# Routing queries without the last norm factor, relu ahead of the split, and lower routing rates

## The chip, the core and the metric

The kernel runs on one core of a Trainium2 chip. The metric is the device time of one execution in microseconds (us). Before the change the median of three runs is 1587.6 us (1587.5 to 1587.79). The engines are TensorE (PE; PEld is its weight load), VectorE (DVE), ScalarE (ACT), GpSimd (POOL), and SyncE (SP), whose queue issues most of the loads.

## What is computed

256 tokens of width 1024 pass three layers. Cut to what matters here:

```python
# layers 0 and 1: attention, layer norm, then
h = layer_norm(ALPHA * h + jnp.square(jax.nn.relu(h @ w_up)) @ w_down)   # width 4096
# layer 0's attention ends with a norm over each head of 128
o = o * lax.rsqrt(jnp.mean(o * o, axis=-1, keepdims=True) + LN_EPS)
# hybrid layer
mixed = concat([rmsnorm(o_a, out_gain_a), rmsnorm(o_b, out_gain_b)]) @ w_out
h = x + mixed
xt = rmsnorm(h, norm2_gain)
# peer: 8 heads, each key 2 x 128 wide, 16384 experts
q = _rms((xt @ w_q).reshape(T, 8, 256))
s1, s2 = q[..., :128] . sub_keys[:, 0], q[..., 128:] . sub_keys[:, 1]
v1, i1 = top_k(s1, 16); v2, i2 = top_k(s2, 16)
vals, ci = top_k(v1[:, None] + v2[None, :], 16)         # 16 experts per head
g = softmax(vals)
y = sum over chosen experts e: g_e * gelu(xt . u_e) * v_e
out = h + y
```

The routing norm divides each query head by its own root mean square, and `rmsnorm(h)` is a factor per token times `h` times a gain per column.

## The kernel before

**Products and blocks.** Every float32 product is made of three matmuls on a high and a low half of each operand (hi*hi, hi*lo, lo*hi). A weight block of 128 x 1024 is loaded by SP's queue into `raw` (four buffers). ACT casts the high half `whi` (L415), and DVE subtracts to get the low half `wlo` (L417); both go to a pool of split blocks, `w` (three buffers) and for the layers up to the hybrid one `wx` (three more). `pump` does that split as soon as a split buffer is free, so the cast of a block waits for the matmuls of an earlier block.

**A projection by features** (`proj_F`, L479) takes eight such blocks, one per 128 columns of the input, and for each issues 24 matmuls of 256 columns: eight hi*hi (L490), then pairs of lo*hi and hi*lo (L494, L495). After each block it calls a hook, pumps, and lets one step of the background list `bg` (`tick`) be issued. Its result fills four PSUM banks of 512 columns. The last block of a group is issued by pairs of outputs, so that the banks end one after another.

**Order.** Each engine takes its instructions in program order. Where the code is plain, that is the order in which the Python lines run. In the hybrid layer `Flow` sets it: many small generators, each added with a rank (`f.add(step, rank)`), say what engine they want next, for how long, and which events they wait for; a list scheduler picks among those that are ready by time and rank, and issues dummy matmuls on PE (L1292, `fill`) where its own estimate finds PE idle.

**Up projection** (`mlp`, L809). Four groups of `proj_F`; at each group's end four banks are relued (ACT, L830), squared (DVE, L831), cast to the high half (ACT, L554) and subtracted (DVE, L555), then `pump` splits the next blocks.

**Sub-norm** (`sub_norm`, L914). Layer 0's attention squares eight pieces of 128 columns on ACT with an accumulator (L920), then takes the root.

**End of the hybrid layer.** `out_dense` (L2030) multiplies the two mixers' outputs with `w_out`: part "b" first, part "a" last, sixteen steps of three matmuls, over four PSUM banks (two token halves th, two column halves i). `last_rms` (L2070) makes the factor `ra` of the first mixer's norm. Then `H.rms` adds the four banks to h (DVE, L2143), squares h on ACT (L2145), makes the root (L382 and what follows it on DVE), scales (`xn`, L2154), transposes on PE (L561, two times eight), and splits the transposed columns into the halves of x by pairs of ACT (L584) and DVE (L585). h is stored to `hscr`.

**Peer** (L2163). Two groups of `proj_F` make the routing queries (P.q). `score_steps`, run from `bg`, scores them against the sub keys and collects the sums of squares `ssq`. Then sixteen groups of `proj_F` (P.U) make xt . u for all experts. In its hooks `routing()` (L2257) issues top-k work on DVE: each step yields a cost, and each hook issues steps until the sum of costs reaches the sum of the rates so far (L2379). In routing stage 0 the low half of the weights is made by POOL (`self.lo_eng = nc.gpsimd`), and by DVE from the end of that stage on. Stage changes hold an exp (L2293) with two table loads on ACT; at each group's end ACT evacuates four banks with Gelu (L2403).

## Time and profile before

| | us |
|---|---|
| median of three runs | 1587.6 |
| profiled execution | 1586.47 |
| its span | 1584.7 |
| PE busy | 1551.7 |
| DVE busy | 1127.3 |
| ACT busy | 823.5 |
| POOL busy | 147.7 |

Busy time is counted from the first to the last moment of an instruction, matmuls that run at half clock included. A row of the list in order of time gives the start, the busy time, the engine, the line, the operation, output and inputs, and a count where equal rows are merged; in brackets stands the idle time before it and what ended that. Stages in us from the start of the span: the sub-norms around 100, the group ends of layer 0's up projection 160 to 230 and of layer 1's up to 542, the hybrid layer 612 to 755, `H.rms` to 766, P.q to about 815, P.U to 1234, and P.V behind it.

### The profile page before, as it was taken

To read this page: it belongs to the slowest core of one execution; us is meant where nothing else is said; L and a number is where in the kernel's file an instruction comes from. 1 tells how busy PE (TensorE), PEld (TensorE's weight loads), DVE (VectorE), ACT (ScalarE), POOL (GpSimd) and SP (SyncE) were. 2 spreads that over 40 slices of the span, in tenths; PEclk is the share of its full clock that TensorE was granted. 3 is DMA by queue.
4 is the path that set the end of the run, shared out by engine and by line. 5 is a ranking of instruction groups with operands and counts; after the bars stand their busy time and mean duration, and the time that the engine had idled before them with its cause. 6 is when DMAs were issued, how large, how long until landed. Compare 5 with 4: busy or idle time off the path is not lost.

```text
span 1584.7 us, 26875 instructions
## 1 busy us (share of the span) xinstructions
PE 1551.7 (98%) x10433; PEld 1393.8 (88%) x10433; DVE 1127.3 (71%) x2172; ACT 823.5 (52%) x1304; POOL 147.7 (9%) x114
## 2 busy tenths in 40 slices
PE   8989999999999999999999998999999999999999
PEld 8879998897799887787999998999999888888887
DVE  5668666586686757777536998778887666666666
ACT  5564555356465654557455444555555544544443
POOL 2000000000200003000027880000000000000000
PEclk9999999999999999999999999999999999999999
DMA  8535768663578695961455775766665777777774
GB/s 295 206 107 173 258 245 286 228 209 124 134 237 292 213 330 205 322 219 49 160 151 184 240 226 190 237 191 209 175 198 176 257 246 246 232 250 237 241 246 153
DMA packets 100306, 339.85 MB, mean 214 GB/s; under 512 B 11121, under 2 KB 16577, under 8 KB 100177
## 3 DMA queue, kind: packets, MB, share of 16 engines
q1 hardware_dynamic: 91216, 310.09, 59.6%
q10 hardware_dynamic: 5760, 18.58, 3.0%
q0 software_dynamic: 3200, 9.45, 2.1%
q8 instruction: 82, 1.34, 0.3%
q14 instruction: 48, 0.39, 0.1%
HBM read 303.74 MB, written 34.34 MB: 213 GB/s over the span
## 4 chain that ended last, share of the span: by engine, by line
PE 71%; DVE 15%; DMA 5%; ACT 5%; issue 2%; SPq 0%; ACTq 0%; DVEq 0%
PE ps L475 13%; PE ps L477 13%; PE ps L476 13%; PE ps L490 9%; PE ps L494 9%; PE ps L495 9%; DVE wlo L417 2%; PE ps L2344 2%; ACT whi L415 2%; DMA ahead<-w_in 1%; DVE t L2253 1%; DMA pre<-ahead 1%; DVE t L2248 1%; DVE t L2251 1%; DVE t L2250 1%
## 5 line engine op out<-in xcount | busy, mean ns | idle before, releaser
L415 ACT CAST whi<-raw 128x1024 fp32r<-128x1024 f32 (+1 forms) x454 | 473.2, 1050 | 498.9 <-PE ps L477 205.2
L417 DVE TENSOR_TENSOR wlo<-raw,whi 128x1024 fp32r<-128x1024 f32 x410 | 498.3, 1223 | 289.4 <-ACT whi L415 288.7
L494 PE MATMUL ps<-x,wlo 128*128 128x256 f32 x1920 | 476.8, 284 | 4.7 <-DVE wlo L417 4.5
L495 PE MATMUL ps<-x,whi 128*128 128x256 f32 x1920 | 476.1, 284 | 0.0
L494 PEld LDWEIGHTS ps<-x,wlo 128*128 128x128 f32 x1920 | 369.2, 192 | 5.7 <-DVE wlo L417 5.7
L495 PEld LDWEIGHTS ps<-x,whi 128*128 128x128 f32 x1920 | 369.4, 192 | 0.0
L490 PE MATMUL ps<-x,whi 128*128 128x256 f32 x1920 | 290.9, 287 | 10.1 <-ACT whi L753 5.9
L475 PE MATMUL ps<-whi,x 128*128 128x512 f32 (+1 forms) x738 | 290.1, 393 | 0.8 <-ACT x L554 0.5
L477 PE MATMUL ps<-whi,x 128*128 128x512 f32 (+1 forms) x738 | 286.2, 388 | 1.5 <-DVE x L1376 1.4
L476 PE MATMUL ps<-wlo,x 128*128 128x512 f32 (+1 forms) x738 | 285.6, 387 | 0.3 <-DVE wlo L420 0.3
L490 PEld LDWEIGHTS ps<-x,whi 128*128 128x128 f32 x1920 | 254.0, 192 | 11.8 <-ACT whi L753 5.9
L475 PEld LDWEIGHTS ps<-whi,x 128*128 128x128 f32 x738 | 138.6, 188 | 34.1 <-issue 5.3
L477 PEld LDWEIGHTS ps<-whi,x 128*128 128x128 f32 x738 | 138.6, 188 | 32.3 <-DVE x L1376 2.6
L476 PEld LDWEIGHTS ps<-wlo,x 128*128 128x128 f32 x738 | 138.7, 188 | 27.7 <-DVE wlo L420 0.6
L417 POOL TENSOR_TENSOR wlo<-raw,whi 128x1024 fp32r<-128x1024 f32 x44 | 106.6, 2422 | 71.2 <-ACT whi L415 71.1
L476 PE MATMUL ps<-wlo,hid 128*128 128x512 f32 x256 | 100.8, 394 | 0.2 <-DVE wlo L417 0.2
L477 PE MATMUL ps<-whi,hid 128*128 128x512 f32 x256 | 100.6, 393 | 0.0
L475 PE MATMUL ps<-whi,hid 128*128 128x512 f32 x256 | 100.6, 393 | 0.0
L476 PEld LDWEIGHTS ps<-wlo,hid 128*128 128x128 f32 x256 | 48.1, 188 | 11.6 <-DVE wlo L417 0.7
L475 PEld LDWEIGHTS ps<-whi,hid 128*128 128x128 f32 x256 | 48.1, 188 | 10.9
L477 PEld LDWEIGHTS ps<-whi,hid 128*128 128x128 f32 x256 | 48.1, 188 | 10.8
L2358 DVE TENSOR_TENSOR oh<-iota,rt 128x1024 f16<-128x1024 f16 x64 | 44.1, 690 | 16.5 <-PE ps L2344 16.3
(397 smaller groups left out, 1462.3 us busy)
## 6 DMA issues: line engine op xcount, KB each, us to landing
raw<-peer_uT SPq DMA_DIRECT2D x128, 512.0 KB, 3.7
raw<-peer_v SPq DMA_DIRECT2D x128, 512.0 KB, 4.3
raw<-w_up SPq DMA_DIRECT2D x64, 512.0 KB, 5.1
raw<-w_down SPq DMA_DIRECT2D x64, 512.0 KB, 5.0
spill<-ga SPq DMA_DIRECT2D x30, 512.0 KB, 6.1
ga<-spill SPq DMA_DIRECT2D x30, 512.0 KB, 5.4
raw<-w_in_a SPq DMA_DIRECT2D x23, 512.0 KB, 5.7
raw<-w_kv SPq DMA_DIRECT2D x16, 512.0 KB, 5.2
```

Of the source, the lines that this page charges most:

```text
L415: (self.hi_eng or nc.scalar.copy)(out=hi[:, :n], in_=raw[:, :n])
L417: eng.tensor_tensor(out=lo[:, :n], in0=raw[:, :n], in1=hi[:, :n], op=ALU.subtract)
L475: mm(out=out, lhsT=lh, rhs=rh, start=start, stop=False, skip_group_check=skip)
L476: mm(out=out, lhsT=lh, rhs=rl, start=False, stop=False, skip_group_check=skip)
L477: mm(out=out, lhsT=ll, rhs=rh, start=False, stop=stop, skip_group_check=skip)
L490: mm(out=outs[o], lhsT=hi[:, sl], rhs=xs.hi(k), start=k == 0 and o % 2 == 0, stop=False, skip_group_check=True)
L494: mm(out=outs[o], lhsT=lo[:, sl], rhs=xs.hi(k), start=False, stop=False, skip_group_check=True)
L495: mm(out=outs[o], lhsT=hi[:, sl], rhs=xs.lo(k), start=False, stop=k == K - 1, skip_group_check=True)
L2248: nc.vector.max_index(out=idx[:, 0:8], in_max=vals[:, 0:8], in_values=src)
L2250: nc.vector.match_replace(out=wk, in_to_replace=vals[:, 0:8], in_values=src, imm_value=-HUGE)
L2344: nc.tensor.matmul(out=o, lhsT=oh[:, t // 2, 0, :, t % 2], rhs=b[:, t // 2, i, :, t % 2], start=i == 0, stop=i == 1)
L2358: nc.vector.tensor_tensor(out=oh.rearrange("p q i n t -> p (q i) n t"), in0=iota.unsqueeze(1).to_broadcast([P, 4, P, 2]), in1=rt[:, 0, pr] ...
```

## The change

1. `mlp`: relu and square of bank j are issued before the split of bank j-1, in both layers.
2. `sub_norm`: two squares of 512 columns on ACT and two reductions on DVE in place of eight squares with an accumulator.
3. `Flow`: ranks change; the last two steps of each bank of part "a" are issued bank by bank (`skew`); the four last updates of h are a generator of the flow (`last_update`).
4. `H.rms`: the 26 dummy matmuls of `fill(8.0)` go; the transposes take h without the factor; squares and root come after the split of x, and give `r2`.
5. Peer: queries and sums of squares are made from x without the factor. `ssq` is multiplied by `r2` twice and `rq` once. `row_of_factors`, the first step in `bg`, turns `r2` into a row of factors `rr` (two DVE scalings `rb`, two matmuls, an ACT copy), and in the second query group each pair of x's chunks is joined, multiplied by `rr` and split again in place (`renorm`).
6. `rates` go from (2.6, 1.0, 1.6) to (2.45, 1.0, 1.65).

```diff
@@ -825,11 +825,15 @@
             for g in range(4):
                 self.ahead_on = True
                 acc = self.proj_F(self.xs, hook=pause if g == 3 else None)
-                for j in range(4):
-                    y = mp.tile([P, 512], F32, tag="relu", name="relu", bufs=3)
-                    nc.scalar.activation(out=y, in_=acc[j], func=AF.Relu)
-                    nc.vector.tensor_tensor(out=y, in0=y, in1=y, op=ALU.mult)
-                    self.split_x(hid, g * 8 + 2 * j, 2, y.rearrange("p (c t) -> p c t", t=S))
+                ys = []
+                for j in range(5):
+                    if j < 4:
+                        y = mp.tile([P, 512], F32, tag="relu", name="relu", bufs=3)
+                        nc.scalar.activation(out=y, in_=acc[j], func=AF.Relu)
+                        nc.vector.tensor_tensor(out=y, in0=y, in1=y, op=ALU.mult)
+                        ys.append(y)
+                    if j:
+                        self.split_x(hid, g * 8 + 2 * (j - 1), 2, ys[j - 1].rearrange("p (c t) -> p c t", t=S))
...
@@ -913,20 +917,17 @@
 
             def sub_norm(hg):
                 ss = self.st.tile([P, 2, 4], F32, tag="ss", name="ss", bufs=2)
+                ns = [ap.tile([P, 512], F32, tag="on", name="on", bufs=4) for _ in range(2)]
                 for th in (1, 0):
-                    for h in range(4):
-                        junk = ap.tile([P, P], F32, tag="junk", name="junk", bufs=2)
-                        ol = o[hg][th][:, h * P:(h + 1) * P]
-                        nc.scalar.activation(out=junk, in_=ol, func=AF.Square, accum_out=ss[:, th, h:h + 1])
+                    nc.scalar.activation(out=ns[th], in_=o[hg][th], func=AF.Square)
+                    nc.vector.tensor_reduce(out=ss[:, th], in_=ns[th].rearrange("p (h d) -> p h d", d=P), axis=AX.X, op=ALU.add)
                 r = self.st.tile([P, 2, 4], F32, tag="sr", name="sr", bufs=2)
                 self.rsqrt_act(r.rearrange("p a b -> p (a b)"), ss.rearrange("p a b -> p (a b)"), LN_EPS, 1.0 / P)
-                ns = []
                 for th in range(2):
-                    n = ap.tile([P, 512], F32, tag="on", name="on", bufs=4)
+                    n = ns[th]
                     nc.vector.tensor_tensor(
                         out=n.rearrange("p (h d) -> p h d", d=P), in0=o[hg][th].rearrange("p (h d) -> p h d", d=P),
                         in1=r[:, th].unsqueeze(2).to_broadcast([P, 4, P]), op=ALU.mult)
-                    ns.append(n)
...
-            f.add(out_dense("a", range(4), end - 4, a_last), 5)
-            f.add(mla_update(), 7.5)
-            f.add(last_rms(), 8)
+            f.add(out_dense("a", range(4), end - 4, a_last), 4.5)
+            f.add(mla_update(), 6.5)
+            f.add(last_rms(), 3.5)
+            f.add(last_update(), 4.5)
...
             def out_dense(which, ks, b, last):
-                for n, k in enumerate(ks):
-                    for th in range(2):
-                        for i in range(2):
-                            ev = yield on_pe(0.69, (ready[b], ms_ev[k]) + ((upd_ev,) if which == "a" else ()),
-                                             1 if n == 0 else 0)
-                            if n == 0:
-                                accs.setdefault(which, [[], []])[th].append(self.bank())
-                            self.step_T(accs[which], ms[0], k, block(b), [0, 512, 1024], th, i, n == 0, n == len(ks) - 1)
-                            last[th, i].t = ev.t if n == len(ks) - 1 else None
-                    release(b, ev)
-                    b += 1
+
+                nk = len(ks)
+                four = [(th, i) for i in range(2) for th in range(2)]
+                skew = 2 if which == "a" else 0
+                seq = [(n, *p) for n in range(nk - skew) for p in four] + [(n, *p) for p in four for n in range(nk - skew, nk)]
+                acc = accs[which] = [[None, None], [None, None]]
+                for n, th, i in seq:
+                    k = ks[n]
+                    ev = yield on_pe(0.69, (ready[b + n], ms_ev[k]) + ((upd_ev,) if which == "a" else ()), 1 if n == 0 else 0)
+                    if n == 0:
+                        acc[th][i] = self.bank()
+                    self.step_T(acc, ms[0], k, block(b + n), [0, 512, 1024], th, i, n == 0, n == nk - 1)
+                    last[th, i].t = ev.t if n == nk - 1 else None
+                    if (th, i) == four[-1]:
+                        release(b + n, ev)
...
+            def last_update():
+                for i in range(2):
+                    for th in range(2):
+                        ev = yield on_dve(512, (a_last[th, i], ra_ev))
+                        sl = slice(i * 512, (i + 1) * 512)
+                        stt(out=new[th][:, sl], in0=accs["a"][th][i], scalar=rbox[0][:, th:th + 1], in1=new[th][:, sl],
+                            op0=mult, op1=add)
+                        accs["a"][th][i] = None
+                        f.give(1, ev)
...
-            fill(8.0)
             del spare
             del self.free[self.wx]
             self.turns = False
-            ra, acc = rbox.pop(), accs.pop("a")
             banks = [self.bank() for _ in range(4)]
-            sss = []
-            for th in range(2):
-                h = self.hs[th]
-                ss = self.st.tile([P, 2], F32, tag="h2s", name="h2s", bufs=2)
-                sss.append(ss)
-                for i in range(2):
-                    sl = slice(i * 512, (i + 1) * 512)
-                    stt(out=h[:, sl], in0=acc[th][i], scalar=ra[:, th:th + 1], in1=h[:, sl], op0=mult, op1=add)
-                    junk = self.res.tile([P, D], F32, tag="lnbcb", name="rjunk")[:, :512]
-                    act(out=junk, in_=h[:, sl], func=AF.Square, accum_out=ss[:, i:i + 1])
-            for th in range(2):
-                h, ss = self.hs[th], sss[th]
-                st = self.st.tile([P, 1], F32, tag="h2t", name="h2t", bufs=2)
-                tt(out=st, in0=ss[:, 0:1], in1=ss[:, 1:2], op=add)
-                r = self.st.tile([P, 1], F32, tag="lnr", name="lnr", bufs=2)
-                self.rsqrt_act(r, st, EPS, 1.0 / D)
-                n = self.res.tile([P, D], F32, tag=f"ln{th}", name="xn")
-                for sl in (slice(0, 256), slice(256, 1024)):
-                    ts(out=n[:, sl], in0=h[:, sl], scalar1=r, scalar2=None, op0=mult)
-                self.t_half(banks, n, th, KD)
+            for c in range(KD):
+                for th in range(2):
+                    o = (c % 2) * S + th * P
+                    nc.tensor.transpose(out=banks[c // 2][:, o:o + P], in_=self.hs[th][:, c * P:(c + 1) * P], identity=self.ident)
+
             self.xs = self.xs_tiles()
             self.t_split(self.xs, banks, KD, gain=lambda c: self.vec("norm2", c))
+            ss = self.const.tile([P, 2, 2], F32, name="h2s")
+            self.r2 = self.const.tile([P, 2], F32, name="r2")
+            for th in range(2):
+                for i in range(2):
+                    junk = self.res.tile([P, D], F32, tag="lnbcb", name="rjunk")[:, :512]
+                    act(out=junk, in_=self.hs[th][:, i * 512:(i + 1) * 512], func=AF.Square, accum_out=ss[:, i, th:th + 1])
+            tt(out=ss[:, 0], in0=ss[:, 0], in1=ss[:, 1], op=add)
+            self.rsqrt_act(self.r2, ss[:, 0], EPS, 1.0 / D)
...
+                r2 = self.r2
+                rr = up.tile([P, S], F32, tag="t5", name="rr")
+
+                def row_of_factors():
+
+                    rb = up.tile([P, 2, P], F32, tag="oh", name="rb", bufs=2)
+                    for th in range(2):
+                        nc.vector.tensor_scalar(out=rb[:, th], in0=self.ident, scalar1=0.0, scalar2=r2[:, th:th + 1],
+                                                op0=ALU.mult, op1=ALU.add)
+                    yield
+                    ps = self.bank()
+                    for th in range(2):
+                        nc.tensor.matmul(out=ps[:, th * P:(th + 1) * P], lhsT=rb[:, th], rhs=self.ident, start=True, stop=True)
+                    nc.scalar.copy(out=rr, in_=ps[:, 0:S])
+                    yield
+
+                def renorm(k):
+
+                    y = up.tile([P, 2, S], F32, tag="oh", name="y", bufs=2)
+                    nc.vector.tensor_tensor(out=y, in0=self.xs.get(0, k, 2), in1=self.xs.get(1, k, 2), op=ALU.add)
+                    nc.vector.tensor_tensor(out=y, in0=y, in1=rr.unsqueeze(1).to_broadcast([P, 2, S]), op=ALU.mult)
+                    self.split_x(self.xs, k, 2, y)
+
+                chunks = iter(range(KD))
+
+                def consumed():
+                    k = next(chunks)
+                    if k in (1, 3, 5):
+                        renorm(k - 1)
+
+                self.bg.append(row_of_factors())
                 for grp in range(2):
-                    acc = self.proj_F(self.xs)
+                    acc = self.proj_F(self.xs, hook=consumed if grp else None)
+                    if grp:
+                        renorm(6)
                     qT = pq[:, grp, 0:8]
                     self.evac_F(qT, acc)
...
                 def routing():
+                    for th in range(2):
+                        r = r2[:, th:th + 1]
+                        nc.vector.tensor_scalar(out=ssq[:, th], in0=ssq[:, th], scalar1=r, scalar2=r, op0=ALU.mult, op1=ALU.mult)
                     for _ in self.rsqrt_steps(rq.rearrange("p a b -> p (a b)"), ssq.rearrange("p a b -> p (a b)"), EPS, 1.0 / 256):
                         yield 0.1
+                    for th in range(2):
+                        nc.vector.tensor_scalar(out=rq[:, th], in0=rq[:, th], scalar1=r2[:, th:th + 1], scalar2=None, op0=ALU.mult)
...
-                rates = (2.6, 1.0, 1.6)
+                rates = (2.45, 1.0, 1.65)
```

The order of PE's instructions where the hybrid layer ends, before: `ps<-one,osq` are the column sums of the last norm, L475 to L477 one step of `out_dense` or of a late head, L1292 the dummies, L561 the transposes, L490 the first query block.

```order
L2079 MATMUL ps<-one,osq 128x1 x4
...
L475 MATMUL ps<-whi,x 128x512
L476 MATMUL ps<-wlo,x 128x512
L477 MATMUL ps<-whi,x 128x512
L1292 MATMUL ps<-k_c_ident 128x128 x26
L561 MATMUL ps<-k_c_ident,xn 128x128 x16
L490 MATMUL ps<-x,whi 128x256 x8
```

After, with the column sums at L2084 and the transposes of h at L2154; L2257 are the two matmuls on `rb`.

```order
L2084 MATMUL ps<-one,osq 128x1 x4
...
L475 MATMUL ps<-whi,x 128x512
L476 MATMUL ps<-wlo,x 128x512
L477 MATMUL ps<-whi,x 128x512
L2154 MATMUL ps<-k_c_ident,h 128x128 x16
L490 MATMUL ps<-x,whi 128x256 x8
L494 MATMUL ps<-x,wlo 128x256
...
L494 MATMUL ps<-x,wlo 128x256
L495 MATMUL ps<-x,whi 128x256
L2257 MATMUL ps<-k_c_ident,rb 128x128 x2
L490 MATMUL ps<-x,whi 128x256 x8
```

What moved: four sum rows further up by three steps, no dummies, and one run of sixteen transposes; L2257 stands between the second and the third query block.

DVE at the same place, before: L2143 adds the banks to h, L2154 scales, L585 makes the low halves of x, L417 those of the weights.

```order
L1224 TENSOR_TENSOR wlo<-raw,whi 128x1024
L2143 SCALAR_TENSOR_TENSOR h<-ps,fr,h 128x512 x4
L2149 TENSOR_TENSOR h2t<-h2s 128x1
L383 TENSOR_SCALAR ra_xh<-h2t 128x1
L384 RECIPROCAL ra_y<-ra_y 128x1
L386 TENSOR_SCALAR ra_t<-ra_y,ra_xh 128x1
L390 SCALAR_TENSOR_TENSOR lnr<-ra_t,ra_y 128x1
L2154 TENSOR_SCALAR xn<-h,lnr 128x256
...
L2154 TENSOR_SCALAR xn<-h,lnr 128x768
L585 SCALAR_TENSOR_TENSOR x<-ps,k_vecs,x 128x256 x8
L417 TENSOR_TENSOR wlo<-raw,whi 128x1024 x7
```

After: L2099 is the update of h, L2164 to L390 the root `r2` (`r_8238`), L2252 the scalings `rb`.

```order
L2099 SCALAR_TENSOR_TENSOR h<-ps,fr,h 128x512 x4
L1225 TENSOR_TENSOR wlo<-raw,whi 128x1024
L585 SCALAR_TENSOR_TENSOR x<-ps,k_vecs,x 128x256 x8
L2164 TENSOR_TENSOR h2s<-h2s 128x2
L383 TENSOR_SCALAR ra_xh<-h2s 128x2
L384 RECIPROCAL ra_y<-ra_y 128x2
L388 TENSOR_TENSOR ra_t<-ra_y 128x2
L389 TENSOR_TENSOR ra_t<-ra_t,ra_xh 128x2
L390 SCALAR_TENSOR_TENSOR r_8238<-ra_t,ra_y 128x2
L417 TENSOR_TENSOR wlo<-raw,whi 128x1024
L2252 TENSOR_SCALAR rb<-k_c_ident,r_8238 128x128 x2
L417 TENSOR_TENSOR wlo<-raw,whi 128x1024 x6
```

The root's steps now stand behind the split of x, and one weight subtraction stands between them and `rb`.

ACT from the root of the last norm on, after: L584 makes the high halves of x, L2163 squares h, L2168 stores it, L415 casts weights, L2258 copies `rr`.

```order
L382 ACTIVATE ra_y<-fr,eps_165 128x2
L1223 CAST whi<-raw 128x1024
L584 ACTIVATE x<-ps,k_vecs 128x256 x8
L2163 ACTIVATE rjunk,h2s<-h 128x512 x4
L382 ACTIVATE ra_y<-h2s,eps_165 128x2
L2168 DMA hscr<-h 128x1024 x2
L415 CAST whi<-raw 128x1024 x2
L2258 COPY rr<-ps 128x256
L415 CAST whi<-raw 128x1024 x5
```

Squares and root stand behind the split here, and all casts but one behind both. In P.U, POOL's list has 46 subtractions L417 in a row, where it had 44.

## Rows read from the trace of the kernel before

**Rows 1.** The page, busy time by engine: busy us, share of span, instructions.

```profile
PE 1551.7 (98%) x10433; PEld 1393.8 (88%) x10433; DVE 1127.3 (71%) x2172; ACT 823.5 (52%) x1304; POOL 147.7 (9%) x114
```

**Rows 2.** In order of time, hybrid layer's end to third query block (start, busy).

```profile
754.58 0.40 PE L477 MATMUL ps<-whi,x 128*128 128x512 f32 x1
...
758.01 0.63 ACT L2145 ACTIVATE rjunk<-h 128x512 f32<-128x512 f32 x1 [1.95 <-DVE h L2143]
...
769.74 1.13 PE L490 MATMUL ps<-x,whi 128*128 128x256 f32 x8
...
770.35 0.48 ACT L584 ACTIVATE x<-ps,k_vecs 128x256 fp32r<-128x256 f32 x1 [0.58 <-DVE x L585]
...
771.26 1.05 ACT L415 CAST whi<-raw 128x1024 fp32r<-128x1024 f32 x1 [0.43 <-issue]
...
772.62 1.12 PE L490 MATMUL ps<-x,whi 128*128 128x256 f32 x8
```

**Rows 3.** In order of time, PE, first matmuls of blocks in both up projections.

```profile
188.50 1.12 PE L490 MATMUL ps<-x,whi 128*128 128x256 f32 x8
...
193.22 0.97 PE L490 MATMUL ps<-x,whi 128*128 128x256 f32 x6 [1.68 <-ACT whi L415]
...
196.50 0.75 PE L490 MATMUL ps<-x,whi 128*128 128x256 f32 x5
...
491.63 1.12 PE L490 MATMUL ps<-x,whi 128*128 128x256 f32 x8
...
496.68 1.22 PE L490 MATMUL ps<-x,whi 128*128 128x256 f32 x8 [2.01 <-ACT whi L415]
...
501.46 1.11 PE L490 MATMUL ps<-x,whi 128*128 128x256 f32 x8
```

**Rows 4.** In order of time, all engines, the end of the first routing stage.

```profile
946.13 2.61 DVE L2281 TENSOR_TENSOR t<-t 128x256 f32<-128x256 f32 x1
...
954.17 0.41 DVE L2281 TENSOR_TENSOR t<-t 128x256 f32<-128x256 f32 x1
...
962.69 1.21 DVE L417 TENSOR_TENSOR wlo<-raw,whi 128x1024 fp32r<-128x1024 f32 x1
...
963.96 0.58 PE L494 MATMUL ps<-x,wlo 128*128 128x256 f32 x1 [4.48 <-DVE wlo L417]
...
964.66 0.31 ACT L2293 ACTIVATE t<-t 128x128 f32<-128x128 f32 x1 [8.75 <-DVE t L2292]
...
964.98 1.28 ACT L322 ACT_TABLE_LOAD   x1
...
966.27 0.20 ACT L322 ACTIVATE tbl<-one 128x1 f32<-128x1 f32 x1
...
968.27 2.05 ACT L2403 ACTIVATE ga<-ps 128x512 f32<-128x512 f32 x4
...
968.82 1.24 PE L490 MATMUL ps<-x,whi 128*128 128x256 f32 x8
```

**Rows 5.** Stretches: length, busy time of each engine (instructions), granted clock, DMA share, GB/s.

```profile
713.00:745.00 32.00, 31.83 (x238) 23.33 (x237) 29.98 (x133) 24.60 (x88) 1.47 (x2) 1.00 0.17 62
...
773.00:850.00 77.00, 77.00 (x650) 76.93 (x649) 32.93 (x42) 38.62 (x56) 20.38 (x11) 1.00 0.56 175
...
854.00:963.00 109.00, 105.48 (x880) 105.27 (x878) 103.11 (x413) 46.27 (x52) 84.43 (x35) 1.00 0.69 217
...
959.00:970.00 11.00, 6.52 (x36) 6.32 (x35) 9.50 (x25) 5.32 (x9) 0.00 (x0) 0.69 0.22 55
```

**Rows 6.** In order of time, ACT and DVE, a group's end in the first up projection.

```profile
184.30 0.60 ACT L830 ACTIVATE relu<-ps 128x512 f32<-128x512 f32 x1 [0.40 <-ACT ahead L440]
...
184.93 0.69 DVE L831 TENSOR_TENSOR relu<-relu 128x512 f32<-128x512 f32 x1
...
192.13 1.04 ACT L415 CAST whi<-raw 128x1024 fp32r<-128x1024 f32 x1
```

**Rows 7.** Instructions of L920: count, ns min/median/max, first and last start.

```profile
L920 ACT ACTIVATE junk<-ps x8: 279/300/330, 95.0 to 96.8; 128x128 f32<-128x128 f32 x8
```

More of the change, by code (lines that the diff above doesn't have):

```diff
@@ L1490, in dense @@
                                      k == 0, k == 1)
-                        f.add(uq_evac(th, i, acc, ev), 16.5)
+                        f.add(uq_evac(th, i, acc, ev), 12)
                         del acc, w
@@ L1502, in dense @@
                         self.mm3(acc[i], lo.hi(2)[:, halves[th]], lo.lo(2)[:, halves[th]], w[0][:, sl], w[1][:, sl], True, True)
-                    f.add(ukv_evac(th, acc, ev), 2)
+                    f.add(ukv_evac(th, acc, ev), 0)
                     del acc, w
@@ L1545, in lora @@
                 gates_ev.t = ev.t
-                f.add(lora_rms(lss, evs), 34)
+                f.add(lora_rms(lss, evs), 30.5)
                 banks = None
@@ L1623, in mla_norms @@
                         self.scale_heads(kr[th].unsqueeze(1).to_broadcast([P, 4, 32]), r[:, th, kl], mqk[th][:, kl, 64:96])
-                        f.add(mla_heads(8 + 4 * h, th, ev), 3.5)
+                        f.add(mla_heads(8 + 4 * h, th, ev), 3)
                         ev = yield on_dve(384, (ev, rope_ev[1][th]))
                         self.scale_heads(mqk[th][:, hl], r[:, th, hl])
-                        f.add(mla_heads(4 * h, th, ev), 2)
+                        f.add(mla_heads(4 * h, th, ev), 2.5)
             def mla_heads(c, th, ev):
@@ L1726, in mla_values @@
                     if c % 2 == 1:
-                        f.add(mla_out(c, ob, ev), 45)
+                        f.add(mla_out(c, ob, ev), 51)
                         del ob
@@ L1766, in values @@
                 for kv in range(2):
-                    f.add(windows(kv, ev, blk_ev[kv]), 25)
-                f.add(compress(blk_ev), 3.5)
+                    f.add(windows(kv, ev, blk_ev[kv]), 32.5)
+                f.add(compress(blk_ev), 6)
             def windows(kv, ev, out):
@@ L2085, in last_rms @@
                 self.rsqrt_act(ra, s, EPS, 1.0 / 512)
+                ra_ev.t = f.now["DVE"]
                 rbox.append(ra)
+            def last_update():
[7 more added lines that the diff above has]
+                        f.give(1, ev)
             nsa_rank = 3
@@ L2090, in hybrid @@
             for th in range(2):
-                f.add(transposed(th), 6)
+                f.add(transposed(th), 6.5)
                 for c in range(KD):
-                    f.add(x_split(th, c), 9.5)
-            f.add(residual(), 6)
-            f.add(dense(), 9)
-            f.add(self.weights(f, end, 3, ready, done, extra, cw_ev), 20)
-            f.add(lora(), 8)
+                    f.add(x_split(th, c), 8.5)
+            f.add(residual(), 3.5)
+            f.add(dense(), 12.5)
+            f.add(self.weights(f, end, 3, ready, done, extra, cw_ev), 20.5)
+            f.add(lora(), 7)
             f.add(gating(), 23.5)
             for th in range(2):
-                f.add(k_rope(th), 43.5)
-                f.add(q_rope(th), 3.5)
-            f.add(mla_norms(), 8.5)
+                f.add(k_rope(th), 52)
+                f.add(q_rope(th), 13.5)
+            f.add(mla_norms(), 9.5)
             for i in range(8):
@@ L2106, in hybrid @@
                 after = [head_ev[d, th] for d in (c, 8 + c) for th in range(2)] + [exp_ev]
-                f.add(head(ops, after, (m_ev, m_used, mts), i), 8)
-            f.add(mla_values(), 19.5)
+                f.add(head(ops, after, (m_ev, m_used, mts), i), 3)
+            f.add(mla_values(), 16.5)
             f.add(values(), 4)
@@ L2111, in hybrid @@
                 f.add(nsa_evac(th), 26)
-            f.add(nsa_norms(), 3.5)
-            f.add(compressed(), 2.5)
+            f.add(nsa_norms(), 9.5)
+            f.add(compressed(), 2)
             for i in range(0, 16, 2):
@@ L2118, in hybrid @@
                 gate = [[gates[th][:, 4 * g + j, 1 + br:2 + br] for th in range(2)] for g in range(2)]
-                f.add(head_pair(ops, (qk_ev[2], qk_ev[j // 2], gate_ev), (n_ev, n_used, nts), i, gate, nsa_rank), 2.5)
+                f.add(head_pair(ops, (qk_ev[2], qk_ev[j // 2], gate_ev), (n_ev, n_used, nts), i, gate, nsa_rank), 0)
             for j in range(4):
-                f.add(nsa_values(j), 1.5)
-            f.add(out_dense("b", range(4, 8), end - 8, b_last), 66.5)
-            f.add(out_dense("a", range(4), end - 4, a_last), 5)
-            f.add(mla_update(), 7.5)
-            f.add(last_rms(), 8)
+                f.add(nsa_values(j), 4.5)
+            f.add(out_dense("b", range(4, 8), end - 8, b_last), 60)
+            f.add(out_dense("a", range(4), end - 4, a_last), 4.5)
+            f.add(mla_update(), 6.5)
+            f.add(last_rms(), 3.5)
+            f.add(last_update(), 4.5)
             self.xs = None
@@ L2266, in routing @@
                     t4 = up.tile([P, 512], F32, tag="b", name="t4", bufs=2)
-                    t5 = up.tile([P, 256], F32, name="t5")
+                    t5 = up.tile([P, 256], F32, tag="t5", name="t5")
                     cand, wk1, wk2 = v3(t3, 0, 256, 16), t4[:, 0:128], t3[:, 256:512]
```

2 lines of the change are left out of this document (1 added, 1 removed).

## The prediction

> **What bounds the kernel now.** I read the page first: TensorE (PE) is busy 98% of the span [rows 1], so of 1584.7 us some 33 are idle, and the rest can only shrink where PE runs at half clock. Then I asked for PE's gaps and what ended each, and for the start of every block of 24 matmuls, which comes 2.88 us after the one before where nothing disturbs it (769.74 to 772.62, [rows 2]). Three places lie in the reach of the change: the way from the hybrid layer to the routing queries [rows 2], the group ends of the up projection [rows 3], and a stretch at 959 to 969 us where PE waits for the low half of a weight block [rows 4]. Last came the table of stretches [rows 5]: VectorE (DVE) is 94% busy in the attention phase of the hybrid layer (713 to 745), 95% in the first routing stage (854 to 963), and 43% in the query projection and the expert group behind it (773 to 850).
>
> **Up projection.** In layer 0, 188.50 to 193.22 is 4.72 us, 1.84 over the pace, and the next block takes 3.28 (0.40 over); in layer 1, 491.63 to 496.68 is 5.05 (2.17 over), and the block behind it 4.78 (1.90 over), its matmuls at half speed [rows 3]. Together 6.3 us. Both stops end with a cast of ScalarE (ACT). ACT and DVE pass each bank of the group to and fro, relu 184.30, square 184.93, high half, low half, and so on, until ACT gets to a cast at 192.13, 7.83 us after the first relu [rows 6]. PE's split blocks run out before that. In the new order relu and square of the next bank fill the turn-round. ACT's eight passes of 0.62 us and DVE's eight of 0.69, begun 0.63 later, then bound it: ACT is free after about 5.3 us and DVE after about 6.1, some 2.6 us earlier, more than either excess. I take all 6.3 back; if the casts behind it are held by their loads, half.
>
> **Sub-norm.** Eight squares with an accumulator read each follow one another from 95.0 to 96.8 [rows 7], so with the last about 2.1 us. Two 512-wide squares (0.60 as a relu of that width) and the second reduction behind them (about 0.69 as DVE's pass) make 1.9, and one more hand-over. Cost 0, bounds -0.3 to +0.3 for each of the two norms.
>
> **Flow.** Ranks move small steps. The order shows nine output steps before the last norm's four column sums and seven behind them, where twelve and four stood; a step is three matmuls, some 0.69 us (its last starts at 754.58, [rows 2], and the 0.24 to the next matmul is a third). The four last updates of h go ahead of a weight subtraction on DVE. DVE's work in the phase is the same but for that one subtraction (1.2 us), and DVE is near its bound there [rows 5]. The last output step could end 1 us sooner or 2 us later (three steps); I take 0.5 later.
>
> **H.rms to the third query block.** Call T the end of the last output step, 754.82. Before, the third block starts at 772.62, T+17.8: subtraction, updates, squares, norm, transposes, split, with the last split pass at 770.35 [rows 2]. After, the updates come first and the transposes take h itself, done at about T+1.9. Block 0 runs T+1.9 to 4.9 and block 1 to 7.7, each fed by the split, whose last pass ends near T+7.7 (one DVE subtraction of 1.2 us stands ahead of its first low half). Only then ACT makes the four squares, 0.63 and an accumulator read, 0.75 each: T+10.75. The square root ends at T+11.3; store issues and cast come 0.91 behind its start, as they do behind the last split pass now (770.35 to 771.26): T+11.95 to 13.0. Behind `r2` DVE has the fourth block's subtraction, which waits for that cast: T+13.05 to 14.25. Behind that stand the two new `rb` scalings, 0.2 each, and PE has the two `rb` matmuls directly behind block 1, as the order shows. So PE waits from T+7.7 to about T+14.7, and the third block starts at T+15.2, 2.6 us sooner. But a stop of 7 us should bring half speed: behind 4.48 us idle, the 22 matmuls left of a block took 4.86 us where 2.64 is the pace, 2.2 lost [rows 4]; the granted clock over 959 to 970 was 0.69, so most of that ran at 1.2 GHz, the lower of the two levels [rows 5]. And 1.9 were lost behind 2.01 idle [rows 3]. I take 2.3 of the 2.6 away: gain 0.3, bounds -2 (a longer stretch at half speed) and +3 (none). Renormalising in place costs DVE about 2.0 us per two blocks in the second query group, and DVE has 57% of its time free from 773 to 850 [rows 5]: nothing. Without that cover each of the four would hold a block by up to 2 us.
>
> **Routing steps per block.** The lower rate spreads stage 0 over 36 blocks instead of 34. Before, DVE's first subtraction comes at 962.69, PE gets its low half at 963.96 after 4.48 idle, and the next block starts at 968.82 where 961.96 was the pace: 6.86 us lost [rows 4]. With two more subtractions on GpSimd (POOL), PE needs DVE's first one only at 965.8. DVE has four more small scalings in the stage, about 0.2 us each: stage end about 963.4, the subtraction done by 964.6, in time. What is late next is ACT: exp waits for DVE (964.66 is 1.97 behind the subtraction's start, so 965.4), then the Gelu load, 1.28, and now the group's four evacuations, 2.05 [rows 4], stand ahead of the next cast. That cast ends about 970.4, and PE wants it at 967.7: 2.7 us idle, 0.2 for the low half, and about 2 of half clock, as behind 2.01 idle. Loss 4.9, gain 2. The new scalings may also lose their turn: a DVE product that takes 0.41 us alone took 2.61 beside a POOL product [rows 4], and as POOL starts one per block, such a miss costs about a block's time. One full miss makes the loss 7.6, gain -0.7. I take 1.0, bounds -2 and +4.5.
>
> Two rules bear on this step. The Trainium skill, SBUF — State Buffer, section "Who interferes with whom", says that a DVE instruction with two SBUF inputs and a GpSimd instruction that reads SBUF shut each other out for the whole instruction. The 2.61 us against 0.41 agree with it; by the page alone a plain scaling would collide only in a two-port mode, and the loss would stay at 4.9. The Trainium skill, ScalarE: Activation LUTs, section "What ACT_TABLE_LOAD costs", gives about 2.66 us for a switch with its drain. The load at 964.98 took 1.28 and the pass behind it starts at 966.27 [rows 4], so the trace disagrees; by the page the next cast would come 1.4 us later and this gain would be about -0.4.
>
> **Sum.** 6.3 + 0 - 0.5 + 0.3 + 1.0 = 7.1. The profiled execution took 1586.47 us, so 1579.4; the median of the runs, 1587.6, lies 1.1 above it: 1580.5.
>
> **Rivals.**
> - *No half clock behind the two new stops, and no miss at the port.* H.rms gives 2.6 and routing 4: 6.3 - 0.5 + 2.6 + 4 = 12.4, so 1575.2. For it: the block behind the stop of 1.68 us at 193.22 ran nearly at pace. Against: behind 2.01 and 4.48 it did not [rows 3, 4]. Chance 0.22.
> - *PE doesn't wait for `rb`.* If the scalings came in time, only the fourth block would wait, for its cast (T+13.1 where it is T+20.7 now): H.rms 7.6, and 6.3 - 0.5 + 7.6 + 2 = 15.4, 1572.2. The order speaks against it. Chance 0.08.
> - *The up projection is held by loads.* Half of the 6.3 stays: 1583.7. For it: the casts draw on four buffers and each refill comes behind a subtraction. Against: the cast at 192.13 follows its high half at once [rows 6]. Chance 0.1.
> - *Slower: the four new routing scalings each wait for a POOL product.* Four misses of 2.88 us are 11.5 on the engine that ends stage 0; with the half clock some 1.1 us per us reach PE, 12.7 beyond the 4.9, loss 17.6, routing -10.7 and the sum -4.6: 1592.2. From the third miss on the gain is gone. Against it: a miss puts what follows in step with POOL, and a product soon after runs in 0.41. Chance 0.06, and 0.02 for other losses of this size.
> - *The change doesn't do what it says*: the new rate leaves the stop where it was and the wait for `rb` is all loss. 6.3 - 0.5 - 2 - 2 = 1.8, 1585.8. Chance 0.07.
>
> **How the numbers follow.** The forecast has 0.45, and its own range from its bounds is 1575 to 1584.5. For 8 in 10 I go from 1571, just below the second rival, to 1586. A measurement of this kernel tells 0.2%, 3.2 us, from no change, so faster means under 1584.4: the forecast but for its upper edge, and the first three rivals, 0.83. The last rival and that edge make same 0.09; slower 0.08.
>
> **What would show it.** Up: ACT's first cast about 5.3 us after the first relu, and no block over 3.0 us behind 188 and 491. H.rms: transposes within 2 us of T, two blocks, then about 7 us idle of PE ended by DVE's `rb`; full clock behind it makes me wrong by 2. Routing: the stop moves from the last block of its group to the third of the next and is ended by ACT's cast, under 3.5 us; a stop ended by DVE there, or one over 5 us, is the port. Wrong altogether: a last output step over 2 us late, or up blocks still at 4.7 us.

## The result and the profile after

The changed kernel takes 1573.48 us (median of four runs, 1571.57 to 1574.8), the kernel before beside it 1587.69: a ratio of 0.9906, interval 0.9889 to 0.9923. That is 0.9% faster, clear of the noise, and inside the range of 1571 to 1586, but the gain, 14.2 us, is twice the 7.1 that was forecast. The profiled execution after took 1573.45 us with a span of 1571.7, 13.0 less than the span before; the other 1.2 us are that the profiled execution before was itself 1.2 under the median.

Layer 0's and layer 1's up projections first: starts of PE's blocks in order of time, as in [rows 3].

```profile
188.69 1.12 PE L490 MATMUL ps<-x,whi 128*128 128x256 f32 x8
191.56 1.12 PE L490 MATMUL ps<-x,whi 128*128 128x256 f32 x8
...
491.59 1.12 PE L490 MATMUL ps<-x,whi 128*128 128x256 f32 x8
494.47 1.10 PE L490 MATMUL ps<-x,whi 128*128 128x256 f32 x8
```

2.87 and 2.88 us from block to block, and no idle time in brackets. ACT over the same group end as [rows 6]:

```profile
183.96 1.09 ACT L832 ACTIVATE relu<-ps 128x512 f32<-128x512 f32 x2 [0.40 <-ACT ahead L440]
...
189.03 3.90 ACT L415 CAST whi<-raw 128x1024 fp32r<-128x1024 f32 x4
```

The first cast comes 5.07 us after the first relu, where it was 7.83. Next the way from the last output step to the fourth query block, all engines in order of time, against [rows 2]:

```profile
746.43 0.39 PE L477 MATMUL ps<-whi,x 128*128 128x512 f32 x1
...
757.42 0.30 ACT L382 ACTIVATE ra_y<-h2s,eps 128x2 f32<-128x2 f32 x1 [0.23 <-DVE h2s L2164]
...
758.33 1.99 ACT L415 CAST whi<-raw 128x1024 fp32r<-128x1024 f32 x2 [0.61 <-issue]
...
759.41 1.22 DVE L417 TENSOR_TENSOR wlo<-raw,whi 128x1024 fp32r<-128x1024 f32 x1 [0.91 <-ACT whi L415]
760.55 0.47 DVE L2252 TENSOR_SCALAR rb<-k_c_ident,r 128x128 f32<-128x128 f32 x2
...
760.98 1.19 PE L2257 MATMUL ps<-k_c_ident,rb 128*128 128x128 f32 x4 [6.42 <-DVE rb L2252]
761.82 2.05 PE L490 MATMUL ps<-x,whi 128*128 128x256 f32 x8
765.72 1.12 PE L490 MATMUL ps<-x,whi 128*128 128x256 f32 x8
```

The last step ends at T = 746.67. The chain is root, cast, subtraction, `rb`, matmuls on `rb`, and the third block starts at T+15.15 (17.8 before). It takes 3.90 us, 1.02 over the pace of 2.88 us per block. Then the end of the first routing stage, against [rows 4]; the first line is the new scaling of `ssq` at the stage's start.

```profile
843.88 2.32 DVE L2301 TENSOR_SCALAR ssq<-ssq,r 128x8 f32<-128x8 f32 x2
...
953.43 1.21 DVE L417 TENSOR_TENSOR wlo<-raw,whi 128x1024 fp32r<-128x1024 f32 x1
955.40 0.31 ACT L2339 ACTIVATE t<-t 128x128 f32<-128x128 f32 x1 [3.50 <-DVE t L2338]
...
957.12 2.04 ACT L2449 ACTIVATE ga<-ps 128x512 f32<-128x512 f32 x4
959.03 2.96 ACT L415 CAST whi<-raw 128x1024 fp32r<-128x1024 f32 x3
...
960.14 1.21 PE L490 MATMUL ps<-x,whi 128*128 128x256 f32 x8 [2.04 <-ACT whi L415]
...
964.54 1.47 PE L490 MATMUL ps<-x,whi 128*128 128x256 f32 x8
...
967.77 0.40 PE L490 MATMUL ps<-x,whi 128*128 128x256 f32 x2
```

PE now stops ahead of the third block of the next group, for ACT's cast behind exp and four evacuations. From 960.14 two blocks take 4.40 and 3.23: 1.52 and 0.35 over, beside 2.19 late at the start, 4.06 in all where it was 6.86. The granted clock over both stops (third column from the end; the levels are 2.4 GHz, shown as 1, and 1.2), from the table of stretches (the columns as in [rows 5], PE's busy time first), the whole of both and then parts of them:

```profile
745.00:767.00 22.00, 15.58 (x111) 14.82 (x111) 9.96 (x22) 10.89 (x22) 1.06 (x2) 0.84 0.42 142
950.00:970.00 20.00, 17.91 (x135) 17.50 (x134) 15.77 (x29) 10.55 (x14) 0.20 (x1) 0.91 0.56 190
...
757.20:760.90 3.70, 0.00 (x0) 0.00 (x0) 2.47 (x9) 2.29 (x3) 0.00 (x0) 0.50 0.71 283
761.00:763.90 2.90, 2.90 (x14) 2.90 (x15) 1.16 (x2) 0.37 (x1) 1.06 (x2) 0.50 0.64 192
...
962.00:965.30 3.30, 3.30 (x18) 3.30 (x17) 3.30 (x4) 0.52 (x1) 0.00 (x0) 0.50 0.81 261
```

In the wait for `rb` the clock fell to 1.2 GHz while PE stood idle, so only 2.9 us of work ran at that level (761.00 to 763.90). In the routing stop it fell after PE had resumed at 960.14, and 3.3 us of work ran at it.

Where the 13.0 us of the span went, from the same places in both traces, beside the forecast and what each part gave when it was undone alone (next section): first by the medians, then at the same place in that kernel's trace. The medians are good to about 1 us, since the kernel before itself moved between 1586.6 and 1587.7 from one group of runs to the next, and T lies between 745.85 and 746.88 in the traces of nine kernels that are the same up to there.

| | forecast | traces | undone alone | its trace, same place |
|---|---|---|---|---|
| up projections | -6.3 | -7.3 | +8.0 | +6.4 |
| start to the sub-norms and the load behind them | 0 | +0.3 | -0.2 (sub-norm) | |
| layer 1's last up block to T | +0.5 | -1.0 | +0.6 (ranks) | +0.9 |
| T to the fourth query block | -0.3 | -1.6 | -2.7 (norm, with its part in routing) | -1.1 |
| end of routing stage 0 | -1.0 | -2.8 | +4.0 | +3.1 |
| rest | 0 | -0.6 | | |
| sum | -7.1 | -13.0 | | |

### The profile page after: what moved, and what is told of

Read it like the earlier page. It is cut to its first block, busy times and chain, and to the rows that moved or that the text cites. A ratio compares the mean times of both kernels' runs of the same rounds, so it can differ in the third digit from the quotient of the medians.

```text
span 1571.7 us, 26776 instructions
## 1 busy us (share of the span) xinstructions
PE 1541.5 (98%) x10383; PEld 1385.7 (88%) x10383; DVE 1134.1 (72%) x2184; ACT 820.9 (52%) x1280; POOL 152.4 (10%) x116
## 5 line engine op out<-in xcount | busy, mean ns | idle before, releaser
L415 ACT CAST whi<-raw 128x1024 fp32r<-128x1024 f32 (+1 forms) x454 | 473.0, 1050 | 511.5 <-PE ps L477 231.4
L417 DVE TENSOR_TENSOR wlo<-raw,whi 128x1024 fp32r<-128x1024 f32 x408 | 496.0, 1223 | 301.1 <-ACT whi L415 300.6
L490 PE MATMUL ps<-x,whi 128*128 128x256 f32 x1920 | 290.4, 287 | 8.7 <-ACT whi L753 6.0
L475 PE MATMUL ps<-whi,x 128*128 128x512 f32 (+1 forms) x738 | 290.9, 394 | 0.5 <-ACT x L554 0.5
L477 PE MATMUL ps<-whi,x 128*128 128x512 f32 (+1 forms) x738 | 286.7, 388 | 0.8 <-DVE x L555 0.7
L490 PEld LDWEIGHTS ps<-x,whi 128*128 128x128 f32 x1920 | 254.0, 192 | 10.1 <-ACT whi L753 6.0
L475 PEld LDWEIGHTS ps<-whi,x 128*128 128x128 f32 x738 | 139.0, 188 | 33.9 <-issue 5.3
L477 PEld LDWEIGHTS ps<-whi,x 128*128 128x128 f32 x738 | 139.0, 188 | 31.3 <-DVE x L555 2.0
L417 POOL TENSOR_TENSOR wlo<-raw,whi 128x1024 fp32r<-128x1024 f32 x46 | 111.4, 2422 | 75.3 <-ACT whi L415 75.1
L475 PE MATMUL ps<-whi,hid 128*128 128x512 f32 x256 | 100.9, 394 | 0.0
L477 PE MATMUL ps<-whi,hid 128*128 128x512 f32 x256 | 100.6, 393 | 0.0
L477 PEld LDWEIGHTS ps<-whi,hid 128*128 128x128 f32 x256 | 48.0, 188 | 11.5
L475 PEld LDWEIGHTS ps<-whi,hid 128*128 128x128 f32 x256 | 48.0, 188 | 10.9
```

The lines of the kernel that those rows point to most:

```text
L415: (self.hi_eng or nc.scalar.copy)(out=hi[:, :n], in_=raw[:, :n])
L417: eng.tensor_tensor(out=lo[:, :n], in0=raw[:, :n], in1=hi[:, :n], op=ALU.subtract)
L475: mm(out=out, lhsT=lh, rhs=rh, start=start, stop=False, skip_group_check=skip)
L477: mm(out=out, lhsT=ll, rhs=rh, start=False, stop=stop, skip_group_check=skip)
L490: mm(out=outs[o], lhsT=hi[:, sl], rhs=xs.hi(k), start=k == 0 and o % 2 == 0, stop=False, skip_group_check=True)
```

## The experiments

All are edits of the changed kernel, whose median is 1573.48. The theory behind them: each term is a stop of PE at a place that the prediction named, and the forecast fell short by the sizes. The rivals differ from place to place.

**The old order in the up projection.** The five old lines of the diff come back in place of the nine new ones.

> The changed kernel with the old order in the up projection (relu, square, high and low half of one bank, then the next). Theory: the stops at the group ends come back, 3.0 us in layer 0 and 4.3 in layer 1 by the starts of the blocks in the two traces, so 7.3 us longer than the changed kernel: about 1580.8. Rival, the loads of the weights and not the banks' turn-round held the casts: at most half of it comes back, 1577 or less.

Measured: 1581.48 us (ratio to the kernel before 0.9965, interval 0.9952 to 0.9978), 8.0 longer. PE's stops are back, first blocks of both layers:

```profile
192.88 1.21 PE L490 MATMUL ps<-x,whi 128*128 128x256 f32 x8 [1.19 <-ACT whi L415]
...
495.76 1.21 PE L490 MATMUL ps<-x,whi 128*128 128x256 f32 x8 [1.61 <-ACT whi L415]
```

The turn-round held the casts, not the loads. The blocks of the two up projections take 6.4 us longer in this trace, near the 6.3 of the forecast. Of the rest, 1.2 stand between T and the fourth query block: the wait for `rb` is as long as in the changed kernel (6.44 us), but the third block behind it takes 5.04 us at half speed where it took 3.90. So the 8.0 is not all the up projection's.

**The old rates.**

```diff
-                rates = (2.45, 1.0, 1.65)
+                rates = (2.6, 1.0, 1.6)
```

> The changed kernel with the old routing rates (2.6, 1.0, 1.6). Theory: the stop goes back to the last block of its group, ended by DVE's first subtraction, loses 6.9 us as before instead of 4.1: 2.8 us longer, about 1576.3. Rival, the stop's length hangs on where DVE's products fall beside POOL's, not on the rate: within 1 us of the changed kernel, or more than 5 longer.

Measured: 1577.45 us (0.9943, 0.993 to 0.9957), 4.0 longer. PE, in order of time:

```profile
949.27 0.40 PE L490 MATMUL ps<-x,whi 128*128 128x256 f32 x2
954.66 0.58 PE L494 MATMUL ps<-x,wlo 128*128 128x256 f32 x1 [4.99 <-DVE wlo L417]
...
959.29 0.88 PE L490 MATMUL ps<-x,whi 128*128 128x256 f32 x6
```

The stop is back at the last block of its group and ended by DVE; the block takes 10.02 us, 7.14 over, against 4.06 in the changed kernel. The trace gives 3.1 of the 4.0 there. It is the rate.

**The old ranks.** 27 numbers are set back; `last_update` gets rank 8.

> The changed kernel with the 27 old ranks of the hybrid layer's steps; the four last updates stay steps of the flow, at the last norm's old rank 8. Theory: the ranks gave 1.0 us between the end of layer 1's up projection and the last output step, so 1 us longer: 1574.5. Rival (the prediction's step): the ranks cost 0.5 us and the gain came from elsewhere, then 0.5 shorter: 1573.

Measured: 1574.13 us (0.9919, 0.9906 to 0.9933), 0.6 longer, which the times alone can't tell from nothing. The traces can: from layer 1's last up block to T it is 225.60 us before, 224.57 in the changed kernel and 225.50 here. The ranks did not cost, they gave about 0.9; the forecast's 0.5 had the wrong sign.

**`rb` two blocks later.**

```diff
                 def row_of_factors():
+                    yield
+                    yield
                     rb = up.tile([P, 2, P], F32, tag="oh", name="rb", bufs=2)
```

> The changed kernel with the two scalings rb and the two matmuls on them two blocks later. Theory: PE's wait of 6.4 us is for rb, which stands behind the fourth block's subtraction; then PE runs the third block first, waits only for the cast of the fourth (at about 759.5 in the changed kernel's trace, where the fourth block starts at 765.7): 4 to 6 us shorter, the lower end if half speed follows the 2 us stop: 1567.5 to 1569.5. Rival, the chain of squares, root and casts sets the pace anyway: the same time within 1 us.

Measured: 1567.97 us (0.9884, 0.9868 to 0.9899), 5.5 shorter. PE, in order of time:

```profile
758.63 1.21 PE L490 MATMUL ps<-x,whi 128*128 128x256 f32 x8 [2.01 <-ACT whi L415]
762.45 0.68 PE L2259 MATMUL ps<-k_c_ident,rb 128*128 128x128 f32 x4 [0.39 <-DVE rb L2254]
762.89 1.19 PE L490 MATMUL ps<-x,whi 128*128 128x256 f32 x8
```

The wait of 6.42 for `rb` is down to 0.39, and the fourth block waits 2.01 for its cast. The fifth block starts at T+17.03 where it was T+21.93, so the stage gives 4.9 of the 5.5. The order had put PE behind a value that is first used, by DVE's first `renorm`, eight blocks later.

**Dummy matmuls in the wait.** Twice, with n = 54 and n = 26:

```diff
                     ps = self.bank()
+                    for _ in range(n):
+                        nc.tensor.matmul(out=ps[:, 0:P], lhsT=self.ident, rhs=self.ident, start=True, stop=True)
```

> The changed kernel with 54 matmuls of the identity by itself, into the bank that the matmuls on rb then overwrite, put ahead of these two: PE works through its wait of 6.4 us. Theory: the half speed of the third block (3.90 us where 2.88 is the pace) comes from the idle time ahead of it; then it goes, 1.0 us shorter, about 1572.5. Rival: half speed comes whatever PE did in the wait: the same 1573.5, or 1 longer if the added matmuls outlast the wait.

> As the kernel with 54 matmuls of the identity in PE's wait for rb, with 26 (each stands as two rows of 0.11 us in the profile, so 26 take 6.0 us; the 54 took 12.2 and outlasted the wait by 5.4). Theory: they end just ahead of rb, the third block runs at the pace, 1.0 us shorter than the changed kernel: 1572.5. Rival: what counts is not this wait and the time stays at 1573.5.

Measured with 54: 1576.51 us (0.9929, 0.9917 to 0.9941), 3.0 longer; with 26: 1571.11 (0.9898, 0.9881 to 0.9915), 2.4 shorter, though the runs of the two kernels overlap; the stage shows 1.4 of it. PE with 54 and then with 26:

```profile
753.77 12.22 PE L2257 MATMUL ps<-k_c_ident 128*128 128x128 f32 x108
766.20 1.20 PE L490 MATMUL ps<-x,whi 128*128 128x256 f32 x8
769.15 1.12 PE L490 MATMUL ps<-x,whi 128*128 128x256 f32 x8
```

```profile
753.92 5.97 PE L2257 MATMUL ps<-k_c_ident 128*128 128x128 f32 x52
760.44 0.71 PE L2259 MATMUL ps<-k_c_ident,rb 128*128 128x128 f32 x4 [0.55 <-DVE rb L2252]
760.91 1.19 PE L490 MATMUL ps<-x,whi 128*128 128x256 f32 x8
763.85 1.12 PE L490 MATMUL ps<-x,whi 128*128 128x256 f32 x8
```

I had sized the 54 by the row's matmuls, and each instruction stands as two of them, so they ran past `rb` by 5.4 us. In both kernels the third block takes 2.95 us where it took 3.90. The matmuls on `rb` take 0.47 with 26 and took 0.84 (760.98 to 761.82). The granted clock from 745 to 767 is 1.00 with 26, where it was 0.84. So the half speed comes from PE's idle time ahead, and costs 1.0 in the block and 0.4 in front of it.

**Lower rates still.** Rates (2.33, 1.0, 1.75).

> The changed kernel with routing rates (2.33, 1.0, 1.75): exp and its table loads then stand behind two casts of the next group, and not ahead of a group's four evacuations. Theory: the stop of 2.0 us and its half speed, 4.1 us in the changed kernel, are made by exp and the evacuations ahead of the cast, and go: 1569.5. Rival: DVE is as late as the lower rate lets it be, or the higher rate of the last stage makes it late there: 1573 or more.

Measured: 1569.6 us (0.9888, 0.9872 to 0.9903), 3.9 shorter, and PE has no stop there. ACT, in order of time:

```profile
954.98 1.05 ACT L415 CAST whi<-raw 128x1024 fp32r<-128x1024 f32 x1 [1.39 <-issue]
956.05 1.28 ACT L2339 ACT_TABLE_LOAD   x1
958.05 0.31 ACT L2339 ACTIVATE t<-t 128x128 f32<-128x128 f32 x1 [0.72 <-DVE t L2338]
...
959.77 2.02 ACT L415 CAST whi<-raw 128x1024 fp32r<-128x1024 f32 x2
```

Exp stands behind the group's evacuations and two casts now, waits 0.72 for DVE in place of 3.50, and the cast behind it is in time.

**Squares between the split's passes.** `split_gain` is one step of `t_split`.

```diff
             self.xs = self.xs_tiles()
-            self.t_split(self.xs, banks, KD, gain=lambda c: self.vec("norm2", c))
             ss = self.const.tile([P, 2, 2], F32, name="h2s")
             self.r2 = self.const.tile([P, 2], F32, name="r2")
-            for th in range(2):
-                for i in range(2):
+            for c in range(KD):
+                self.split_gain(self.xs, c, banks[c // 2][:, (c % 2) * S:(c % 2 + 1) * S], self.vec("norm2", c))
+                if c % 2 == 0:
+                    th, i = c // 4, c // 2 % 2
                     junk = self.res.tile([P, D], F32, tag="lnbcb", name="rjunk")[:, :512]
                     act(out=junk, in_=self.hs[th][:, i * 512:(i + 1) * 512], func=AF.Square, accum_out=ss[:, i, th:th + 1])
```

> The changed kernel with the four squares of h issued between the split's passes (behind chunks 0, 2, 4 and 6) instead of behind all of them. Theory: ACT has gaps of 0.6 us between its split passes and 1.3 behind the first, so the factor is ready about 1.3 us sooner and the wait for rb ends as much sooner: 1572.2. Rival: the squares hold the split and with it the second block by as much: 1573.5.

Measured: 1570.37 us (0.9893, 0.9876 to 0.9909), 3.1 shorter, twice what I expected, with runs that spread from 1568.54 to 1574.01. PE:

```profile
757.96 1.20 PE L2258 MATMUL ps<-k_c_ident,rb 128*128 128x128 f32 x4 [3.96 <-DVE rb L2253]
```

The wait for `rb` is 2.46 shorter, and the fourth block comes at T+16.53 where it was T+19.05: the trace gives 2.5 of the 3.1. All four squares went into ACT's gaps, and the split ended no later.

**The norm as before, the rest changed.** H.rms has squares, root and scaling ahead of the transposes again, P.q and the routing no `r2`; the updates of h stay in the flow, and no dummies are issued.

> The changed kernel with the norm of h as before (squares, root and scaling ahead of the transposes; no rb, no renormalising, no r2 in the routing), the four last updates of h still steps of the flow and no dummies. Theory: what the stage gained comes from the early updates of h and not from the norm's new place; the first square can start 1.9 us sooner after the last output step than in the kernel before, so the third block comes at T+15.9 where the changed kernel has T+15.2 and 1.0 lost at half speed: 1573.3, within 1 us of the changed kernel. Rival: the norm's new place gave the gain: 1575 or more.

Measured: 1570.74 us (0.9898, 0.9881 to 0.9914), 2.7 shorter than the changed kernel, more than the 1 us that I had allowed, though the intervals of the two ratios overlap. T is 746.88 here. PE at H.rms and at the end of routing stage 0:

```profile
752.43 3.90 PE L561 MATMUL ps<-k_c_ident,xn 128*128 128x128 f32 x16 [5.40 <-DVE xn L2167]
...
761.91 1.12 PE L490 MATMUL ps<-x,whi 128*128 128x256 f32 x8
```

```profile
958.72 1.22 PE L490 MATMUL ps<-x,whi 128*128 128x256 f32 x8 [1.54 <-ACT whi L415]
962.00 1.12 PE L490 MATMUL ps<-x,whi 128*128 128x256 f32 x8
```

With the norm in its old place the third block comes at T+15.03, no later than with the new one, and at full pace, although the sixteen transposes ran at half speed (3.90 us for the row, where the changed kernel has 1.99). The routing stop loses 2.1 us in place of 4.06. Of these 2.0, 0.5 is a shorter wait, since the stage has four scalings less; the rest is half speed, which did not come here (the granted clock from 945 to 965 is 1.00). So the gain in H.rms came from the early updates of h, and the norm's new place, with `rb` where it stood, took back about 1.1 there and 2.0 in the routing, as far as two traces tell.

**The old sub-norm.** The squares with an accumulator come back.

> The changed kernel with the old sub-norm (eight squares with an accumulator read, no reductions). Theory: PE's stops at the two norms get 0.1 us longer each: 1573.7, not to be told from the changed kernel. Rival: squares and reductions trade 1 us or more: 1572.5 or 1574.7.

Measured: 1573.24 us (0.9911, 0.9895 to 0.9928): no difference.

**The three places together**: `rb` three blocks later, squares between the split's passes, rates (2.33, 1.0, 1.75).

> The changed kernel with rb three blocks later, the squares between the split's passes and routing rates (2.33, 1.0, 1.75). If the three places are independent: 5.5 (measured for the later rb) + 1.3 + 4.1 shorter, about 1562.6. If the stops only move (the cast of the fourth block still late, DVE late in the last stage): 1567 to 1569.

Measured: 1561.17 us, 0.9834 of the kernel before (0.9821 to 0.9847), faster than both. PE around `rb`:

```profile
759.56 1.12 PE L490 MATMUL ps<-x,whi 128*128 128x256 f32 x8
762.44 0.65 PE L2261 MATMUL ps<-k_c_ident,rb 128*128 128x128 f32 x4
762.85 1.20 PE L490 MATMUL ps<-x,whi 128*128 128x256 f32 x8
```

No idle time in brackets is left, and 12.3 us come off, 1.4 more than the parts that I had added up (10.9) and as much as the three measured alone (5.5, 3.1 and 3.9): the stops did not move elsewhere.

## Why the prediction was right or wrong

The stops stood and moved where the prediction put them. What failed is the sum: four of its terms were 1.0 to 1.8 us too small, the routing term most, and one of them, the flow, had the wrong sign. The sub-norm's 0.3 the other way is less than such traces scatter.

*Routing* is the term that was mis-sized most: 1.0 forecast, 2.8 by the traces, 3.1 to 4.0 undone. The stop moved to the third block of the next group and is ended by ACT's cast, and exp came 1.97 us after DVE's subtraction, as worked out. The loss without a miss was put at 4.9 (gain 2) and is 4.06. The step that failed is the one behind it: I had taken one more off for a miss beside POOL, and none was added. The first `ssq` scaling did lose its turn (2.32 us for two passes of 0.17, beside a POOL subtraction of 2.40 us from 843.57), but what followed then fell into step: six DVE passes met a POOL product in the stage before (one of 2.01, two of about 2.4 in the root, three products) and six after. From the last copy of `ssq` to DVE's first subtraction the stage is 109.63 us long (843.80 to 953.43), where it was 109.11 (853.58 to 962.69). The Trainium skill, SBUF — State Buffer, section "Who interferes with whom", lists tensor_scalar among the instructions that can take the shared port pair; the 2.32 us agree. In this stage the new miss stood in place of an old one and did not come on top. (The prediction prices a miss at 2.7 us in one place and at 3.2 in the slower rival; neither came.)

*Up projection*: 6.3 forecast, 7.3 by the traces of before and after, 6.4 by the trace with the old order. I had counted the excess of four blocks and left out the small ones behind them. ACT was free after 5.07 us, forecast 5.3.

*H.rms*: the third block at T+15.15, forecast T+15.2, and PE's wait of 6.42 us ended by `rb`, all as worked out from the order. Mis-sized is the price of half speed, 1.4 and not 2.3, of which 0.4 lay inside the T+15.15. I had taken it from two other stops, as if a stop had a price of its own. The runs show that the half speed comes from idle time (the dummies take it away), and that its cost goes by how much work PE does at 1.2 GHz. The same wait stands in two other kernels: 6.44 us with the old up projection, whose rows come first and then the clock of a stretch behind the wait, and 6.43 us with the old rates, of which the last line gives the stretch behind it:

```profile
767.87 1.19 PE L2253 MATMUL ps<-k_c_ident,rb 128*128 128x128 f32 x4 [6.44 <-DVE rb L2248]
768.71 2.05 PE L490 MATMUL ps<-x,whi 128*128 128x256 f32 x8
```

```profile
767.90:773.40 5.50, 5.50 (x26) 5.50 (x27) 1.15 (x2) 0.37 (x1) 1.06 (x2) 0.50 0.78 242
```

```profile
760.60:764.40 3.80, 3.80 (x18) 3.80 (x19) 1.15 (x2) 0.37 (x1) 1.06 (x2) 0.50 0.64 189
```

Behind one and the same wait of 6.4 us, 2.9 us of work at the lower level lost 1.4 in the changed kernel, 3.8 us lost 1.8 with the old rates and 5.5 us lost 2.5 with the old up projection: a little under half each time. The clock fell 2.6, 3.5 and 5.2 us into the wait, and the sooner it fell the more of the slow stretch passed while PE stood idle. Why it fell sooner or later no run shows, so the small loss in the changed kernel is luck as far as these runs tell. Nor did the gain need the norm's new place: with the old one the fourth block comes at T+17.92, where it was T+20.68 before and is T+19.05 after the change.

*Flow*: 0.5 longer forecast, 1.0 shorter by the traces, 0.6 by the old ranks. The sign was a guess from the order; the old ranks bring 0.9 back in the trace, but which rank gave it stays open. That the three fewer steps ahead of the norm would cost was wrong: they ran behind the column sums, which took as long as before.

*The rival that PE doesn't wait for `rb`* was rightly put low. Its 1572.2 is still the nearest in time, 1.3 off, which is luck: PE did wait. *No half clock, no miss*, at 1575.2, is 1.7 off, for half of its reason: no miss. The slower rival's four misses did not come.

What the prediction did not see: part of the change worked against the rest. The price of taking the norm off the path was a new value on PE's path one stage later, and with the updates of h already early the old norm cost less: undone, it took 2.7 us off.

## What to carry to other kernels

When a value is taken off the critical path, look where its first consumer stands in the order of an engine that runs in order: here two small matmuls, needed eight blocks later, held PE for 6.4 us, and two yields removed it. Bound each term from its rows, but don't let every doubt point the same way: four terms, each 1.0 to 1.8 us too small, made a forecast half the size. An evacuation and a table switch ahead of a cast count like the cast itself; moving a stage's end by two blocks was worth 3 to 4 us because of what stood next to it.

## What the runs showed of the hardware

A float32 matmul of the 128 x 128 identity by itself stands as two rows of the profile, 0.23 us for both: 54 took 12.2 us. The length of a stop of PE doesn't tell what it costs: 1.4 us were lost at half speed behind 6.42 us of idle time in the changed kernel, 1.9 behind 2.04 in the same kernel, and 2.5 behind 6.44 with the old up projection. What tells it is the work done while the granted clock is at 1.2 GHz: 2.9, 3.8 and 5.5 us of it lost 1.4, 1.8 and 2.5. On ACT a table load took 1.28 us, with the next pass 0.01 behind it (955.72 and 957.01 in the changed kernel), as before.
